# A hybrid decoder block on one NeuronCore: quarter sums of X by adding transfers, X tiles block-major, and four side pieces placed elsewhere

## The chip, the cores and the metric

The kernel runs on one core of a Trainium2 chip. The core has a matmul engine (PE, TensorE, which reads its stationary operand in a weight-load step, PEld), a vector engine (DVE), a scalar engine (ACT), a general engine (POOL), a queue engine (SP) and sixteen DMA engines. Each engine works through its own list of instructions in order. Transfers are issued from the lists of SP, ACT and POOL; a transfer issued by POOL can add what it brings to what is already at its target. The metric is the device time of one execution, in microseconds.

## The reference, cut to what matters

One layer on 1024 tokens of width 1024, all in float32:

```python
hn = rms_norm(h, norm_mix_g)
proj = hn @ w_in                       # gMLP | RG-LRU | SSD z, xBC, dt | gates
ya = gmlp_mixer(za, ...)               # gelu, layer norm, 128x128 mixing, product
yb = rg_lru_mixer(zb, ...)             # conv 4, gates, scan, gelu gate
yc = ssd_mixer(z, xbc, dt_raw, ...)    # softplus(dt), conv 4, chunked scan, norm
gates = sigmoid(g_raw + b_gate)        # three branches
merged = (gates[0] * (ya @ w_branch_a) + gates[1] * (yb @ w_branch_b)
          + gates[2] * (yc @ w_branch_c))
h = h + merged @ w_out
h = h + relu(rms_norm(h, norm_mlp_g) @ w_mlp_up) ** 2 @ w_mlp_down
return rms_norm(h, final_norm_g)
```

In the SSD mixer, `dt = softplus(dt_raw + dt_bias)` and `adt = dt * a` give the decays of 16 heads over 8 chunks of 128 tokens. For each of 4 groups the output is a product inside a chunk plus a product with the state carried from the chunk before.

## The kernel before, in words

Every float32 operand is split into a high half (rounded) and a low half (the rest), and a product is three matmuls: high by high, low by high, high by low. `split` (L125 to L133) makes the halves: ACT writes the high one (L132), DVE subtracts (L133).

**Start.** The rows of x are normalized and transposed; ACT and DVE write X, the transposed input, as sixteen tiles: two halves, two sets of 512 tokens, four pairs of 128-row blocks. Then the value blocks of gMLP run (`v_block`, L257; DVE L236 and L238 end a gelu), and with them the columns for dt.

**Units.** Then come 48 units (`one_unit`, L558). A unit is 48 matmuls (L555) of a 1024x128 weight tile with X, into one of two PSUM buffers (`mainp`). `wtile` (L521) brings the weights: SP loads `raw` (L523), ACT writes high and negated high (L526, L527), POOL issues a transfer that adds `raw` to the latter (L528). Weights are asked for two units ahead. After each unit its `post` reads the PSUM buffer, and `step` advances each waiting generator to its next `yield`. The order of units is four SSD groups of six, each followed by four of the RG-LRU (two heads), then eight of gMLP.

The generators carry the side work. `dt_stages` computes the decays: a softplus on DVE (L218 to L230), adt (L595, L596), then the cumulated sums on TensorE (L601, L602). `ssd_stages` runs a group in two halves of 512 tokens: s1 transposes, s2 states (DVE L720 carries them on), s3 outputs (L729 with the state, L733 inside the chunk; DVE L736 to L739), s4 norm (L746 to L758). The RG-LRU's gate products are L813; their operand is split by L132 and L133. gMLP mixes in L857, L858 evicts, POOL multiplies (L860) and stores (L861).

**Gate pairs.** The 24 blocks of gate columns are made in twelve pairs by a seven-product scheme (Strassen-Winograd): p1 to p7, each of 12 matmuls (`seventh`, L478), on quarters of X and sums of them. T1, T2, T3, T4 are these sums. `x_forms` (L875 to L914) computes them during the gMLP units, with DVE, from high and low quarters (L892 to L905), and splits them. T3 goes back into a quarter of X that is no longer needed. Weight sums and splits of a pair are `Weights` (L484 to L516). The pairs' order is written by hand in `tc.manual_schedule()`.

**Branch products, out projection, MLP.** The branch products are 24 units on Y, the mixers' outputs brought back from memory (`fetch`, `load_next`). Then the weights of the out projection are loaded and split, and for each two row blocks TensorE makes L1142; the rows of x for the residual come by a transfer from ACT's list (L1148), and DVE adds (L1155). Norm, the MLP in the same seven-product scheme, and the final norm follow.

Outside `tc.manual_schedule()` a scheduler of the framework sets the order of each engine's list, with a model of its own for times; the program order is its start. Tiles come from pools of a fixed number of slots (`act` 15, `half` 16, `raw` 2), and an instruction that writes a tile waits until the slot is free.

## Time and profile before

| | us |
|---|---|
| median of 3 runs (2023.78 to 2027.23) | 2026.16 |
| the profiled execution | 2023.37 |
| its span | 2021.7 |
| TensorE busy | 1959.3 (97%) |
| VectorE busy | 1219.6 (60%) |
| ScalarE busy | 944.5 (47%) |
| GpSimd busy | 326.6 (16%) |
| mean granted clock of TensorE | 0.988 |

So 1.7 us of the profiled execution lie outside its span, and the median is 2.8 above it. In the rows of a profile, `out<-in` names what an instruction writes and reads, `xN` counts the instructions of a row, and `[t <-X]` behind a row is idle time of the engine before it and what ended that. In rows of `windows`, busy time of PE, PEld, DVE, ACT and POOL stands in this order, then the granted clock, the mean busy share of the sixteen DMA engines, and GB/s.

### The profile page before, as it was taken

The page shows a single profiled execution, that of the slowest core. Times are in us where ns is not written, and L with a number is a line of the kernel's source. Part 1 is how long each engine was busy: PE and PEld are TensorE (multiplying, and loading weights), DVE is VectorE, ACT ScalarE, POOL GpSimd, SP SyncE. Part 2 cuts the span into 40 slices and gives each one's busy share as a digit, 9 for nine tenths or more (in the row PEclk, how much of TensorE's full clock was granted, in tenths as well). Part 3 has the DMA queues.
Part 4 walks back from the last instruction along what each step waited for, and adds up shares of the span by engine and source line. Part 5 has one row for each costly group of instructions (what it writes and reads, how often), then busy time and mean ns, then how long its engine had stood idle before and what let it go on. Part 6 is the DMA issues. An engine that isn't in the chain of part 4 may idle for free.

```text
span 2021.7 us, 23919 instructions
## 1 busy us (share of the span) xinstructions
PE 1959.3 (97%) x9156; PEld 1633.8 (81%) x9156; DVE 1219.6 (60%) x1796; ACT 944.5 (47%) x1377; POOL 326.6 (16%) x410
## 2 busy tenths in 40 slices
PE   7999999999999999999999999998999999999996
PEld 7997878788788787888878888786788887888885
DVE  5486775765867778444432113336756657787787
ACT  6434665656556534344443222146555555343243
POOL 4112231231322333000000320000111111000000
PEclk9999999999999999999999999999999999999998
DMA  4256456456265564333496665421543448644532
GB/s 157 67 152 129 103 131 138 102 116 129 73 147 119 125 167 134 106 109 114 146 321 186 157 155 136 156 84 63 166 155 132 166 145 309 199 135 136 187 106 92
DMA packets 214887, 285.54 MB, mean 141 GB/s; under 512 B 12548, under 2 KB 149972, under 8 KB 214772
## 3 DMA queue, kind: packets, MB, share of 16 engines
q1 hardware_dynamic: 175636, 144.91, 23.9%
q0 software_dynamic: 33200, 117.59, 22.4%
q10 hardware_dynamic: 5936, 21.51, 3.2%
q8 instruction: 72, 1.18, 0.2%
q14 instruction: 43, 0.35, 0.1%
HBM read 178.97 MB, written 67.24 MB: 122 GB/s over the span
## 4 chain that ended last, share of the span: by engine, by line
PE 78%; DVE 13%; ACT 3%; DMA 3%; issue 2%; POOL 0%; SPq 0%; DVEq 0%; ACTq 0%; POOLq 0%
PE ps L555 32%; PE aux L478 30%; PE gps L478 6%; PE aux L257 3%; PE aux L1142 2%; DVE a L578 1%; PE aux L729 1%; PE aux L733 1%; PE aux L813 1%; DVE rsq_q L111 1%; DMA raw<-in_w_branch_c_dram 1%; DMA a<-in_x_dram 1%; ACT a L1183 1%; DVE a L828 1%; DVE h L750 1%
## 5 line engine op out<-in xcount | busy, mean ns | idle before, releaser
L555 PE MATMUL ps<-xn,wh 128*128 128x512 f32 x1536 | 418.3, 392 | 0.0
L555 PEld LDWEIGHTS ps<-xn,wh 128*128 128x128 f32 x1536 | 286.9, 188 | 61.1 <-issue 2.8
L555 PE MATMUL ps<-xn,wl 128*128 128x512 f32 x768 | 236.6, 389 | 0.0
L478 PE MATMUL aux<-a,b 128*128 128x512 f32 x864 | 197.3, 389 | 0.0
L478 PEld LDWEIGHTS aux<-a,b 128*128 128x128 f32 x864 | 162.2, 188 | 33.7
L526 ACT ACTIVATE wh<-raw 128x1024 fp32r<-128x1024 f32 x72 | 76.0, 1056 | 228.4 <-PE ps L555 201.8
L555 PEld LDWEIGHTS ps<-xn,wl 128*128 128x128 f32 x768 | 144.2, 188 | 30.1
L478 PE MATMUL aux<-b,wt 128*128 128x512 f32 x672 | 156.9, 389 | 0.0
L478 PEld LDWEIGHTS aux<-b,wt 128*128 128x128 f32 x672 | 126.1, 188 | 26.2
L528 POOL DMA_DIRECT2D wl<-raw x72 | 64.0, 889 | 416.4 <-ACT wl L527 248.6
L478 PE MATMUL aux<-b,b 128*128 128x512 f32 x480 | 110.6, 389 | 0.0
L1037 DVE SCALAR_TENSOR_TENSOR a<-a,ps 128x1024 f32<-128x1024 f32 x22 | 26.8, 1220 | 137.9 <-PE ps L555 115.3
L133 DVE TENSOR_TENSOR wt<-a,wt 128x1024 fp32r<-128x1024 f32 x52 | 63.7, 1225 | 72.6 <-ACT wt L132 72.6
L1364 DVE TENSOR_TENSOR a<-aux,a 128x512 f32<-128x512 f32 x112 | 76.8, 687 | 50.5 <-PE aux L478 50.5
L478 PEld LDWEIGHTS aux<-b,b 128*128 128x128 f32 x480 | 90.1, 188 | 18.7
L133 DVE TENSOR_TENSOR a<-a,a 128x1024 fp32r<-128x1024 f32 (+1 forms) x65 | 66.7, 1032 | 47.1 <-ACT a L132 47.0
L132 ACT ACTIVATE b<-wt 128x1024 fp32r<-128x1024 f32 x60 | 61.9, 1053 | 69.6 <-DMA wt<-u_d 53.8
L555 PE MATMUL ps<-c,wh 128*128 128x512 f32 x320 | 85.5, 389 | 0.0
L478 PE MATMUL aux<-a,wt 128*128 128x512 f32 x336 | 78.7, 390 | 3.3 <-ACT a L1241 3.3
L132 ACT ACTIVATE a<-a 128x1024 fp32r<-128x1024 f32 (+1 forms) x65 | 55.8, 875 | 55.5 <-DVE a L1316 44.2
L478 PEld LDWEIGHTS aux<-a,wt 128*128 128x128 f32 x336 | 62.9, 188 | 17.2 <-ACT a L1241 4.2
L527 ACT ACTIVATE wl<-wh 128x1024 fp32r<-128x1024 f32 x72 | 75.7, 1052 | 0.8
(333 smaller groups left out, 3726.1 us busy)
## 6 DMA issues: line engine op xcount, KB each, us to landing
wl<-raw POOLq DMA_DIRECT2D x72, 512.0 KB, 5.2
wt<-u_d SPq DMA_DIRECT2D x54, 512.0 KB
raw<-in_w_in_dram SPq DMA_DIRECT2D x48, 512.0 KB
u_d<-a POOLq DMA_DIRECT2D x48, 512.0 KB, 5.5
g_d<-a POOLq DMA_DIRECT2D x24, 512.0 KB, 2.9
a<-g_d ACTq DMA_DIRECT2D x22, 512.0 KB
rt<-in_w_mlp_up_dram SPq DMA_DIRECT2D x17, 512.0 KB
a<-acs_d POOLq DMA_DIRECT2D x32, 256.0 KB, 7.6
```

The costliest lines, as they stand in the source:

```text
L111: stt(out=q, in0=r, scalar=nh, in1=r, op0=ALU.mult, op1=ALU.mult)
L132: actv(dst_hi, src, AF.Copy)
L133: (eng or nc.vector).tensor_tensor(out=dst_lo, in0=src, in1=dst_hi.bitcast(F32), op=ALU.subtract)
L257: mm(ps[:, :nt], X.tok(a, k, c), wk[k][w], start=(k == 0 and i == 0), stop=(k == KD - 1 and i == 2))
L478: mm(ps, lhs[l][kk], rhs[r][kk], start=(new and n == 0), stop=(n == 11), skip_group_check=not new)
L526: actv(hi, raw, AF.Copy)
L527: actv(lo, hi.bitcast(F32), AF.Copy, scale=-1.0)
L528: nc.gpsimd.dma_start(out=lo, in_=raw, accum_op=ALU.add)
L555: mm(ps[:, hsl(h)], w[wi][:, k, :], a.rhs(ai, k, h), start=(n == 0), stop=(n == 3 * KD - 1))
L1037: stt(out=t, in0=t, scalar=1.0, in1=ps, op0=ALU.add, op1=ALU.mult)
L1142: mm(ps, M.tok(a, k, c), wo[nb][k][w], start=(k == 0 and a + w == 0), stop=(k == KD - 1 and a == 1))
L1364: tt(out=h, in0=ps, in1=h, op=ALU.add)
```

## The change

1. **X tiles** are laid out block by block, (pair's block, token block, token), so that the 512 tokens of one block are contiguous (`tile`, `rhs`, `tok`).
2. **Decays.** The first stage of `dt_stages` is called before the units, not after the first, and one `yield` of two is gone.
3. **SSD outputs.** One more `yield` stands between s2(1) and s3(1) of a group.
4. **x_forms.** T2, T1 and T4 start as copies of a high quarter (six transfers on SP's list), the low quarter is added by transfers on POOL's list (six), T3 to T2 (two), and the negated T2 to T1 and T4 (four). DVE keeps three additions or subtractions for each of T3's two tiles, and the splits; ACT negates T2. T3's split runs once the queue of units is empty, ahead of the last stage.
5. **Branch c.** The second weight tile of the branch products is asked for in the last gate pair behind p6, not in the loop that loads the fourth to eighth block of Y.
6. **Residual rows.** The first two row blocks of x are asked for ahead of the split of the out projection's weights. 25 slots of the pool are passed over, so that the rows lie in slots 25 and 26 of 27.

```diff
--- before.py
+++ after.py
@@ -139,14 +139,14 @@
 
         def tile(self, part, half, kp):
             if (part, half, kp) not in self.t:
-                self.t[part, half, kp] = self.new[half % len(self.new)]((P, 4, 2, P), F32R)
+                self.t[part, half, kp] = self.new[half % len(self.new)]((P, 2, 4, P), F32R)
             return self.t[part, half, kp]
 
         def rhs(self, part, k, half):
-            return self.tile(part, half, k // 2)[:, :, k % 2, :]
+            return self.tile(part, half, k // 2)[:, k % 2]
 
         def tok(self, part, k, c):
-            return self.tile(part, c // 4, k // 2)[:, c % 4, k % 2, :]
+            return self.tile(part, c // 4, k // 2)[:, k % 2, c % 4]
 
     class Whole:
         def __init__(self, hi, lo):
@@ -164,12 +164,12 @@
 
     def x_high(ps, c, q):
         for k in range(4 * q, 4 * q + 4):
-            actv(X.tile(0, c // 4, k // 2)[:, c % 4, k % 2], ps[q][:, k % 4 * P:(k % 4 + 1) * P], AF.Identity, scale=g2c[:, k:k + 1])
+            actv(X.tok(0, k, c), ps[q][:, k % 4 * P:(k % 4 + 1) * P], AF.Identity, scale=g2c[:, k:k + 1])
 
     def x_low(ps, c, q):
         for k in range(4 * q, 4 * q + 4):
-            stt(out=X.tile(1, c // 4, k // 2)[:, c % 4, k % 2], in0=ps[q][:, k % 4 * P:(k % 4 + 1) * P], scalar=g2c[:, k:k + 1],
-                in1=X.tile(0, c // 4, k // 2)[:, c % 4, k % 2].bitcast(F32), op0=ALU.mult, op1=ALU.subtract)
+            stt(out=X.tok(1, k, c), in0=ps[q][:, k % 4 * P:(k % 4 + 1) * P], scalar=g2c[:, k:k + 1],
+                in1=X.tok(0, k, c).bitcast(F32), op0=ALU.mult, op1=ALU.subtract)
 
...
@@ -595,7 +595,6 @@
         ts(out=adt, in0=dt, scalar1=-1.0, scalar2=None, op0=ALU.mult)
         tt(out=adt, in0=adt, in1=na.unsqueeze(1).to_broadcast([P, NCH, 16]), op=ALU.mult)
         yield
-        yield
         adt_f = adt.rearrange("p c h -> p (c h)")
         ps_a = aux()
         mm(ps_a[:, :P], tri, adt_f, start=True, stop=True)
@@ -614,7 +613,9 @@
         nc.gpsimd.dma_start(out=acs_d.rearrange("t r l -> r t l"), in_=acsT)
         yield
 
-    later(dt_stages())
+    decays = dt_stages()
+    next(decays)
+    later(decays)
 
 
     def ssd_units(g):
@@ -770,6 +771,7 @@
         s4_(0)
         yield
         s2_(1)
+        yield
         yield
         s3_(1)
         yield
@@ -871,47 +873,64 @@
 
     XF = {n: [[X.rhs(part, 4 * kh + kk, th) for kk in range(4)] for part in range(2)]
           for n, kh, th in (("B11", 0, 0), ("B21", 1, 0), ("B22", 1, 1), ("T3", 0, 1))}
+    XF.update({n: [[], []] for n in ("T1", "T2", "T4")})
 
     def x_forms():
-        third = []
-        for n in ("T1", "T2", "T4"):
-            XF[n] = [[None] * 4, [None] * 4]
+
+        def quarter(part, kh, th, kp):
+            return X.tile(part, th, 2 * kh + kp).bitcast(F32)
+
+        def plus(out, in_):
+            nc.gpsimd.dma_start(out=out, in_=in_, accum_op=ALU.add)
+
+        def in_halves(name, kp):
+            for k in range(2):
+                pr = half_((P, 4, P), F32R), half_((P, 4, P), F32R)
+                split(pr[0], pr[1], sums[name][kp][:, k])
+                for part in range(2):
+                    XF[name][part].append(pr[part])
+
+
+        first_of = {"T2": (0, 0), "T1": (1, 1), "T4": (1, 0)}
+        sums = {n: [act((P, 2, 4, P)) for _ in range(2)] for n in first_of}
+        for n, (kh, th) in first_of.items():
+            for kp in range(2):
+                nc.sync.dma_start(out=sums[n][kp], in_=quarter(0, kh, th, kp))
+        t3 = []
         for kp in range(2):
-            def quarter(part, kh, th):
-                return X.tile(part, th, 2 * kh + kp).bitcast(F32)
-
-            def in_halves(name, t):
-                for kk in range(2):
-                    pr = half_(dt=F32R), half_(dt=F32R)
-                    for part in range(2):
-                        XF[name][part][2 * kp + kk] = pr[part]
-                    split(pr[0].rearrange("p (c l) -> p c l", c=4), pr[1].rearrange("p (c l) -> p c l", c=4), t[:, :, kk, :])
-
-            third.append(act((P, 4, 2, P)))
-            t3, d, e = third[kp], act((P, 4, 2, P)), act((P, 4, 2, P))
-            tt(out=t3, in0=quarter(0, 1, 1), in1=quarter(0, 0, 1), op=sub)
-            tt(out=e, in0=quarter(1, 1, 1), in1=quarter(1, 0, 1), op=sub)
-            tt(out=t3, in0=t3, in1=e, op=ALU.add)
+            d = act((P, 2, 4, P))
+            tt(out=d, in0=quarter(0, 1, 1, kp), in1=quarter(0, 0, 1, kp), op=sub)
+            tt(out=d, in0=d, in1=quarter(1, 1, 1, kp), op=ALU.add)
+            tt(out=d, in0=d, in1=quarter(1, 0, 1, kp), op=sub)
+            t3.append(d)
             yield
-            tt(out=d, in0=quarter(0, 0, 0), in1=t3, op=ALU.add)
-            tt(out=d, in0=quarter(1, 0, 0), in1=d, op=ALU.add)
-            in_halves("T2", d)
+        for n, (kh, th) in first_of.items():
+            for kp in range(2):
+                plus(sums[n][kp], quarter(1, kh, th, kp))
+        yield
+        for kp in range(2):
+            plus(sums["T2"][kp], t3[kp])
+        yield
+        for kp in range(2):
+            in_halves("T2", kp)
+            actv(sums["T2"][kp], sums["T2"][kp], AF.Copy, scale=-1.0)
+            plus(sums["T1"][kp], sums["T2"][kp])
+            plus(sums["T4"][kp], sums["T2"][kp])
+        yield
+        yield
+        for kp in range(2):
+            in_halves("T1", kp)
+        yield
+        for kp in range(2):
+            pr = act((P, 2, 4, P), F32R), act((P, 2, 4, P), F32R)
+            split(pr[0], pr[1], sums["T4"][kp])
+            for part in range(2):
+                XF["T4"][part] += [pr[part][:, k] for k in range(2)]
+        sums.clear()
+        while queue:
             yield
-            tt(out=e, in0=quarter(0, 1, 1), in1=d, op=sub)
-            tt(out=e, in0=quarter(1, 1, 1), in1=e, op=ALU.add)
-            in_halves("T1", e)
-            yield
-            tt(out=d, in0=quarter(0, 1, 0), in1=d, op=sub)
-            tt(out=d, in0=quarter(1, 1, 0), in1=d, op=ALU.add)
-            pr = act((P, 4, 2, P), F32R), act((P, 4, 2, P), F32R)
-            split(pr[0], pr[1], d)
-            for part in range(2):
-                for kk in range(2):
-                    XF["T4"][part][2 * kp + kk] = pr[part][:, :, kk, :]
-            yield
-        assert not queue
         for kp in range(2):
-            split(X.tile(0, 1, kp), X.tile(1, 1, kp), third[kp])
+            split(X.tile(0, 1, kp), X.tile(1, 1, kp), t3[kp])
 
     class GatePair:
         def __init__(self, br, e):
@@ -1081,6 +1100,7 @@
             else:
                 early.append(fetch("c", 2))
                 load_next("c", 0, early[0])
+                ahead(2)
             z.p3()
             if nxt:
                 nxt.w.cast22()
@@ -1104,8 +1124,6 @@
         early = [fetch("c", k) for k in range(3, KD)]
         for k in range(3, KD):
             load_next("c", k, early[k - 3])
-            if k == 5:
-                ahead(2)
         one_unit()
     del early
     run()
@@ -1121,6 +1139,18 @@
         return aux2p.tile([P, HF], F32, tag="aux2", name=nm("aux2"))
 
 
+
+    skipped = [act() for _ in range(25)]
+    H = []
+
+    def residual(c):
+        h = act()
+        nc.scalar.dma_start(out=h, in_=x[c * P:(c + 1) * P, :])
+        H.append(h)
+
+    for c in range(2):
+        residual(c)
+    del skipped
     wo = [[], []]
     for nb in range(2):
         for k2 in range(4):
@@ -1129,7 +1159,6 @@
             hi, lo = w_pair(nb == 0 and k2 < 3)
             split(hi, lo, raw)
             wo[nb] += [(hi[:, k, :], lo[:, k, :]) for k in range(2)]
-    H = []
     NF = w_up.shape[1] // P
     NS = NF // 2
     h_d = dram.tile([NCH, P, D], F32, name="h_d")
@@ -1143,10 +1172,9 @@
 
     for cp in range(NCH // 2):
         pss = [aux(), aux()]
-        for i in range(2):
-            h = act()
-            nc.scalar.dma_start(out=h, in_=x[(2 * cp + i) * P:(2 * cp + i + 1) * P, :])
-            H.append(h)
+        if cp:
+            for i in range(2):
+                residual(2 * cp + i)
         for ks in (range(KD - 1), (KD - 1,)):
             for i in range(2):
                 out_products(pss[i], 0, 2 * cp + i, ks)
```

The change's lines stand two lines further down from L597 on (L729 is L730 there, L813 is L815, L858 is L860), and more behind `x_forms`.

TensorE at the end of the tenth unit of an SSD and RG-LRU stretch, before (the 128x128 and 64x128 rows are the SSD outputs, L813 the gate products):

```order
L555 MATMUL ps_2508<-xn_555,wl_2227 128x512
L729 MATMUL aux_2563<-a_1741,h_2096 128x128 x2
L733 MATMUL aux_2564<-a_2218,h_2297 64x128 x2
L729 MATMUL aux_2563<-a_1741,h_2489 128x128
L733 MATMUL aux_2564<-a_2218,h_2297 64x128 x2
L733 MATMUL aux_2564<-a_2221,h_2306 64x128 x4
L729 MATMUL aux_2583<-a_1741,h_2096 128x128
...
L555 MATMUL ps_2658<-xn_224,wh_2408 128x512
L555 MATMUL ps_2658<-xn_537,wh_2408 128x512
L813 MATMUL aux_2605<-h_2474,lw_2470 128x512
L813 MATMUL aux_2605<-h_2475,lw_2470 128x512
```

And with the change:

```order
L555 MATMUL ps_2508<-xn_555,wl_2227 128x512
L815 MATMUL aux_2564<-h_2474,lw_2470 128x512
L815 MATMUL aux_2564<-h_2475,lw_2470 128x512
L815 MATMUL aux_2564<-h_2474,lw_2471 128x512
...
L555 MATMUL ps_2617<-xn_224,wh_2408 128x512
L815 MATMUL aux_2592<-h_2478,lw_2470 128x512
...
L555 MATMUL ps_2617<-xn_555,wl_2409 128x512
L730 MATMUL aux_2674<-a_1755,h_2096 128x128 x2
L730 MATMUL aux_2674<-a_1755,h_2489 128x128 x2
L734 MATMUL aux_2675<-a_2218,h_2297 64x128 x4
```

The outputs of the second half of a group stand a whole unit later, and the gate products L815, which stood behind them, now stand where they were.

DVE in the last two gMLP units, before (a_6234 becomes T4, a_6235 is T1, xn_543 takes T3; L502 to L506 are sums of gate weights):

```order
L133 TENSOR_TENSOR xn_543<-a_5900,xn_537 128x1024
L133 TENSOR_TENSOR h_6398<-a_6235,h_6397 128x512
L904 TENSOR_TENSOR a_6234<-xn_239,a_6234 128x1024
L236 SCALAR_TENSOR_TENSOR a_6390<-a_6390,ps_6340 128x1024
L133 TENSOR_TENSOR h_6402<-a_6235,h_6401 128x512
L905 TENSOR_TENSOR a_6234<-xn_246,a_6234 128x1024
L238 SCALAR_TENSOR_TENSOR a_6389<-a_6390,ps_6340 128x1024
L502 TENSOR_TENSOR a_6409<-a_6337 128x512
L503 TENSOR_TENSOR a_6410<-rt_6336,a_6337 128x512
L506 TENSOR_TENSOR a_6409<-a_6409,rt_6336 128x512
L858 SCALAR_TENSOR_TENSOR a_6415<-aux_6416,vh,bs 128x512
```

With the change:

```order
L133 TENSOR_TENSOR xn_543<-a_5898,xn_537 128x1024
L133 TENSOR_TENSOR xn_546<-a_5980,xn_540 128x1024
L236 SCALAR_TENSOR_TENSOR a_6392<-a_6392,ps_6342 128x1024
L238 SCALAR_TENSOR_TENSOR a_6391<-a_6392,ps_6342 128x1024
L502 TENSOR_TENSOR a_6417<-a_6339 128x512
L503 TENSOR_TENSOR a_6418<-rt_6338,a_6339 128x512
L506 TENSOR_TENSOR a_6417<-a_6417,rt_6338 128x512
L860 SCALAR_TENSOR_TENSOR a_6423<-aux_6424,vh,bs 128x512
L507 TENSOR_TENSOR a_6418<-rt_6338,a_6417 128x512
L860 SCALAR_TENSOR_TENSOR a_6423<-aux_6430,vh,bs 128x512
L133 TENSOR_TENSOR a_6439<-a_5890,a_6438 128x1024
L133 TENSOR_TENSOR a_6443<-a_5891,a_6442 128x1024
```

The sums L904 and L905 and T1's splits between L236 and L238 are gone, T3's second split has come in ahead of L236, and two splits of T4 (a_5890, a_5891) stand behind the two L860.

POOL's list early in the gMLP units, with the change (L884 are the adding transfers, xn the low quarters, a_5898 and a_5980 the two tiles of T3):

```order
L863 DMA ya_d<-a_5871 128x1024
L884 DMA a_5886<-xn_230 128x1024
L884 DMA a_5887<-xn_233 128x1024
...
L884 DMA a_5891<-xn_246 128x1024
L528 DMA wl_6002<-raw_5999 128x1024
L845 DMA a_5964<-vn_d 128x8x128
L884 DMA a_5886<-a_5898 128x1024
L884 DMA a_5887<-a_5980 128x1024
L528 DMA wl_6087<-raw_6084 128x1024
```

Before, the list went from ya_d to yc_d, wl and vn_d with none of the L884 rows. Now the transfer that adds the low half of a weight tile (wl_6002) stands behind six of them, and the next (wl_6087) behind the two that add T3 to T2.

## The prediction

> **What bounds the kernel now.** I read the page first, then the list of what TensorE waited for, then the timelines around each wait.
>
> ```profile
> PE 1959.3 (97%) x9156; PEld 1633.8 (81%) x9156; DVE 1219.6 (60%) x1796; ACT 944.5 (47%) x1377; POOL 326.6 (16%) x410
> ```
>
> TensorE (PE) is busy 1959.3 of 2021.7 us. An edit that leaves the matmuls alone can win only idle time, 62 us, and stretches at a lowered clock. These waits are the ones the edits aim at (total, times, longest):
>
> ```profile
> PE aux L729 <- DVE h L720: 8.1, 4, 2.2
> ...
> PE aux L478 <- DVE a L858: 4.5, 1, 4.5
> ...
> PE aux L601 <- DVE adt L596: 2.1, 1, 2.1
> PE aux L1142 <- DVE a L1155: 1.9, 1, 1.9
> PE ps L555 <- DMA wl<-raw: 1.7, 1, 1.7
> ```
>
> They sum to 18.3 us. The rest of the idle time (start, norm chain, tail) is not touched.
>
> **The change part by part**
>
> **X block-major.** The moving operand of the units becomes contiguous. Units on X and branch products, whose operand is contiguous already, stand in the groups (count, busy, mean ns):
>
> ```profile
> L555 PE MATMUL ps<-xn,wh 128*128 128x512 f32 x1536 | 418.3, 392 | 0.0
> ...
> L555 PE MATMUL ps<-c,wh 128*128 128x512 f32 x320 | 85.5, 389 | 0.0
> ```
>
> 392 against 389 ns, and matmuls overlap (a unit's 48 take 10.90 us in a row below, 227 ns each). I take no gain. Were the 3 ns real, 0.8%, the 1536 of this row at 227 ns would win 0.008 × 349 = 2.7 us: the upper end.
>
> **SSD outputs a product later.** At the end of each of four groups TensorE runs two first outputs, waits for the state update L720, then does the rest at a clock that fell in most groups (PE and DVE timelines, then 2-us windows whose last three columns are clock, DMA share, GB/s):
>
> ```profile
> 254.01 0.60 PE L729 MATMUL aux<-a,h 128*128 128x128 f32 x4
> ...
> 264.10 0.62 PE L555 MATMUL ps<-xn,wh 128*128 128x512 f32 x2
> ```
>
> ```profile
> 389.35 0.60 PE L729 MATMUL aux<-a,h 128*128 128x128 f32 x4
> ...
> 392.27 0.77 PE L729 MATMUL aux<-a,h 128*128 128x128 f32 x2 [1.95 <-DVE h L720]
> ...
> 400.74 0.62 PE L555 MATMUL ps<-xn,wh 128*128 128x512 f32 x2
> ```
>
> ```profile
> 390.54 1.29 DVE L133 TENSOR_TENSOR h<-a,h 128x512 fp32r<-128x512 f32 x2 [0.76 <-ACT h L132]
> 391.75 1.61 DVE L720 SCALAR_TENSOR_TENSOR h<-h,etot,aux 128x64 f32<-128x64 f32 x8
> ```
>
> ```profile
> 394.00:396.00 2.00, 2.00 (x14) 1.67 (x11) 0.79 (x2) 1.99 (x2) 0.86 (x1) 0.56 0.12 18
> ...
> 530.00:532.00 2.00, 2.00 (x16) 1.67 (x13) 1.15 (x2) 1.97 (x3) 0.86 (x1) 0.50 0.34 64
> ...
> 666.00:668.00 2.00, 2.00 (x15) 1.45 (x15) 1.75 (x5) 1.98 (x3) 0.61 (x2) 0.50 0.61 113
> ```
>
> The same matmuls took 264.10 − 254.01 = 10.09 us in the first group, at full clock, and 400.74 − 389.35 = 11.39 in the second, although its wait was 0.28 shorter (2.23, the longest, against 1.95). So the lowered clock costs 1.3 + 0.28, about 1.6 us, in three groups of four: 4.8. With the waits' 8.1 the place costs 12.9 in all.
>
> The wait does not simply go. The program order puts the gate products L813 of the RG-LRU at that spot, and they need the low halves that DVE writes just ahead of L720: L133 x2, 390.54 to 391.83. The pair takes about 0.65 each, so the first half stands at 391.2 and the second at 391.8. TensorE arrives at 389.35, waits about 1.9, does six matmuls of about 0.23 (1.4) and waits at most 0.4 for the second. Per group that is a wait of 1.9, at most 2.2, for 1.95 to 2.23 before: 0 to 0.3 won. If DVE reaches L133 sooner than before, up to the whole wait goes: 8.1.
>
> The clock is the larger part. The gap now has matmuls of 512 columns on both sides instead of outputs of 128 columns. Where a gap of this size had wide matmuls around it (L601's and L1142's), the clock held; and the same outputs without a wait, in a group's first half, ran at 1.00 too:
>
> ```profile
> 160.00:162.00 2.00, 0.96 (x6) 0.92 (x7) 1.19 (x3) 1.46 (x2) 0.00 (x0) 1.00 0.00 0
> ```
>
> ```profile
> 1300.00:1302.00 2.00, 1.45 (x6) 1.21 (x7) 1.18 (x2) 0.00 (x0) 0.00 (x0) 1.00 1.02 406
> ```
>
> ```profile
> 210.00:212.00 2.00, 2.00 (x26) 1.71 (x25) 1.45 (x2) 2.00 (x3) 0.00 (x0) 1.00 0.69 206
> ```
>
> I take two of the three drops away: 3.2, with bounds 0 and 4.8. Together 3.8 (bounds 0 to 12.9; and 1 lost, if the moved outputs meet full DVE work a unit later).
>
> The Trainium skill ("TensorE: Matmul & The Clock Gate", its section on the HAM clock gate) has the clock halve after at least one idle window of about 3.4 us and asks for no gaps above that. By it the 1.95-us gap should have cost no clock; the 0.56 after it speaks against the plain reading. By the rule alone this part would win 0.6, not 3.8.
>
> **Sums of quarters by transfers.** The last gMLP outputs are late and two gate products wait for them:
>
> ```profile
> 783.09 5.42 PE L478 MATMUL aux<-xn,wt 128*128 128x512 f32 x12 [4.48 <-DVE a L858]
> ```
>
> ```profile
> 784.00:786.00 2.00, 2.00 (x6) 1.52 (x6) 2.00 (x3) 0.00 (x0) 1.61 (x1) 0.50 0.52 130
> ```
>
> ```profile
> 776.49 1.21 DVE L236 SCALAR_TENSOR_TENSOR a<-a,ps 128x1024 f32<-128x1024 f32 x1
> ...
> 782.30 0.74 DVE L858 SCALAR_TENSOR_TENSOR a<-aux,vh,bs 128x512 f32<-128x512 f32 x1
> ```
>
> The 12 matmuls at clock 0.50 took 5.42, twice what they take at full clock, so the place costs 4.48 + 2.7 = 7.2. The adds that stood before L236 leave DVE, so L236 can start when ScalarE has its input, nearly 2 us sooner. L238, three weight sums and L858 still follow in that order: p2 gets free near 780.6 and waits about 2.1. Then p5 needs S1, whose low half stands on DVE behind L507, L858 and two splits of T4 that have moved there: about 1.5 more. With some chance of the clock falling (0.8 as an estimate), 4.4 remain: 2.8 won (bounds: 7.2 won, if DVE is early enough; losses below).
>
> Its price is 18 transfers of 512 KB.
>
> ```profile
> q1 hardware_dynamic: 175636, 144.91, 23.9%
> q0 software_dynamic: 33200, 117.59, 22.4%
> ...
> wl<-raw POOLq DMA_DIRECT2D x72, 512.0 KB, 5.2
> ```
>
> ```profile
> 700.00:730.00 30.00, 30.00 (x150) 25.45 (x149) 28.76 (x27) 12.33 (x15) 12.62 (x11) 1.00 0.67 174
> ```
>
> 483 us for 144.91 MB is 3.3 us per MB of all sixteen engines on SP's queue, 3.85 on POOL's. Six copies (3.1 MB) and twelve accumulations (6.3 MB) make 10.5 + 24.2 = 35 us in a stretch whose share is 0.67 already. None lies on TensorE's path by itself; what hides them is this slack:
>
> ```profile
> 698.67 0.37 SPq L523 DMA_DIRECT2D raw<-in_w_in_dram  x1
> ```
>
> ```profile
> 727.74 1.21 DVE L236 SCALAR_TENSOR_TENSOR a<-a,ps 128x1024 f32<-128x1024 f32 x1
> ...
> 730.61 1.21 DVE L238 SCALAR_TENSOR_TENSOR a<-a,ps 128x1024 f32<-128x1024 f32 x1
> ```
>
> ```profile
> 736.05 10.90 PE ps L555 x48
> ```
>
> The copies stand on SP behind the load issued at 698.67. T2's first split stands on DVE between this L236 and this L238. TensorE has two PSUM buffers for units, so the unit at 736.05 needs that L238, ended 731.8: 4.2 us of slack. T2 needs a copy, an accumulation and, after T3, a second one; one that accumulates takes 5.2 us to land (the wl<-raw row). T3's first half needs DVE near 719, the second near 727, since SSD's norm (L750 to L757, eight ops and some 8 us) has moved into that stretch. First T2 near 726 to 732, with DVE itself up to 4 us late: just inside the slack. I charge 0.5.
>
> **Decays earlier.** DVE's softplus (25 ops, about 7 us) moves from after the third unit to before the first.
>
> ```profile
> 143.02 3.91 DVE L578 SCALAR_TENSOR_TENSOR a<-ps,scw,a 128x1023 f32<-128x1023 f32 x3
> ...
> 149.51 0.95 DVE L222 RECIPROCAL a<-a 128x128 f32<-128x128 f32 x1
> ...
> 160.70 0.28 DVE L596 TENSOR_TENSOR adt<-adt,na 128x128 f32<-128x128 f32 x1
> ```
>
> ```profile
> 112.00:160.00 48.00, 44.32 (x133) 1.00 0.50 151
> 105.00:112.00 7.00, 3.33 (x10) 1.00 0.54 141
> ```
>
> L601's 2.1 goes. DVE is 92% busy from 112 to 160, with 3.7 us free before it: these absorb their share and 3.3 push all that follows. The first unit's convolution releases its PSUM at 146.9 (143.02 + 3.91). The third unit, which needs it, ended with the wait of L601 at 161.0 − 2.1, so it began at 148.0: slack 1.1, and 0.7 more for decay products that now stand in front. 3.3 − 1.8 is a new stop of 1.5; the value blocks, with no slack that I find, lose 0.3. Net 0.3 won (2.1 won to 2 lost).
>
> **Second branch-c weight.** Now a request late behind others takes 15 us:
>
> ```profile
> 1002.53 15.00 DMA raw<-in_w_branch_c_dram
> ```
>
> Asked for a gate product earlier, it lands in time: 1.7 won, less 0.4 (an estimate) since its two casts stand ahead of a split on ScalarE that the last product wants. 1.3 (0 to 1.7).
>
> **Residual rows.** They are asked for ahead of five weight casts instead of behind them:
>
> ```profile
> 1294.19 5.16 DMA a<-in_x_dram
> ```
>
> Any start 2 us sooner takes away the wait: 1.9 (0 to 1.9; behind it stand the casts, with several us to spare).
>
> **Sum.** 0 + 3.8 + 2.8 − 0.5 + 0.3 + 1.3 + 1.9 = 9.6 us. The profiled execution took 2023.4, so it would take 2013.8. The median shown is 2026.2, 2.8 above it; from there, 2016.6. I forecast 2015.5. A measurement of this kernel tells about 0.2% (4 us) from no change.
>
> **The rivals**
>
> *The clock is not the gap's.* If the drop at the group ends has another cause, or L813 behind a gap brings it too, the 3.2 stay lost: 9.6 − 3.2 = 6.4, about 2019. For it: the drop shows in three of four groups and not at the two other gaps of 2 us. Against: the outputs without a wait stayed at full clock. Chance 0.13. The Trainium skill ("TensorE: Matmul & The Clock Gate", HAM clock gate), read strictly, gives this time as well.
>
> *The gate products' wait vanishes too.* DVE does L133 before TensorE asks; then this place gives its full 12.9 instead of 3.8: near 2006. Against it: what releases L133 is ScalarE's L132, unchanged. Chance 0.06.
>
> *Waits are only exchanged.* L813 waits and the clock falls as before, p2 and p5 give 1, decays lose 1.5, the two requests win 3.2: 2 to 3 us, about 2023, not to be told from no change. Chance 0.17.
>
> *T2 comes late (slower).* The shares of the 16 engines leave about 10 us free from 700 to 730, and copies and accumulations that stand ahead of T2 in the queues want up to 27 (six copies 10.5, eight accumulations 16). If T2's half comes after 733, DVE is held with L238 and the gMLP outputs behind it, and TensorE stops one for one. At 746 that is 13 us, and a lowered clock for 2.7 as at p2; the 2.3 of this part is not won. 9.6 − 2.3 − 13 − 2.7 is 8 us slower, near 2033. From 738 on the whole is no faster than before (9.6 − 2.3 − 2.7 = 4.6 against 738 − 733 = 5). For it: the queues in order (a weight's accumulation on POOL stands behind six others). Against: first copies and first accumulations are T2's own, and other traffic yields too. Chance 0.2.
>
> **Chances.** The forecast has 0.44. Faster: 0.44 + 0.13 + 0.06 = 0.63; same: 0.17; slower: 0.20. Faster cases reach from 2006 to 2021. The range, 2005 to 2030, leaves out the worst of the late T2 and little at the fast end; the forecast's own is 2010 to 2021.
>
> **What would show it.** Right: no wait of L601 on L596, of L555 on an accumulated weight near 1027, of L1142 on L1155; at the group ends a wait of L813 on L133 of 1.5 to 2 us, followed by a clock of 1.00; p2's wait near 2. Wrong: four waits at L813 with a clock of 0.5 behind them; a stop at units between 730 and 765 that ends with a split or L238; the value blocks or the first units waiting on L578; longer casts of weights.

## The result and the profile after

The change took 2034.39 us (median of 5 runs, 2032.85 to 2037.58) against 2026.16 before (5 runs, 2023.78 to 2027.68). The ratio is 1.0044, with a 95% interval of 1.003 to 1.0059: slower by 0.44%, outside the range of the prediction and on its unlikely side. The profiled execution has a span of 2032.6 us, 10.9 more than before. The page says that TensorE did nearly the same work:

```profile
PE 1962.2 (97%) x9156; PEld 1632.6 (80%) x9156; DVE 1200.9 (59%) x1784; ACT 957.4 (47%) x1387; POOL 339.0 (17%) x422
```

Of the five waits that the edits aimed at, four have left its list and p2's has shrunk from 4.5 to 1.0 (the L860 row). Others have come (L815 is L813 of before, L609 the transpose of the decays' sums, L859 gMLP's mixing, L860 is L858, L1056 is L1037):

```profile
PE ps L555 <- DVE a L238: 8.1, 2, 8.0
...
PE aux L815 <- ACT h L132: 4.3, 4, 1.1
PE aux L609 <- DVE w L606: 4.2, 1, 4.2
PE aux L859 <- DMA a<-vn_d: 4.0, 1, 4.0
...
PE ps L555 <- DVE a L1056: 1.7, 1, 1.7
...
PE aux L478 <- DVE a L860: 1.0, 1, 1.0
PE aux L815 <- DVE h L133: 0.9, 4, 0.2
```

The length of each stage, from the starts of its first matmuls in the two PE timelines, tells where the 10.9 us came from:

| stage | before | after | difference |
|---|---|---|---|
| to the first unit | 126.09 | 125.75 | −0.3 |
| units of SSD and RG-LRU | 569.97 | 567.36 | −2.6 |
| gMLP units, to the first pair's p1 | 79.57 | 97.20 | +17.6 |
| the first pair | 15.47 | 11.53 | −3.9 |
| other pairs, to the first branch product | 222.38 | 223.42 | +1.0 |
| branch products | 263.30 | 263.29 | 0.0 |
| out projection to the end | 744.92 | 744.03 | −0.9 |

One stage lost 17.6 us. There the sixteen DMA engines were full: the next rows are 700 to 770 us of the profile before and of the one after (columns as before; the last three are clock, DMA share, GB/s; the view prints shares a little above 1 where the engines are full).

```profile
700.00:770.00 70.00, 70.00 (x351) 59.47 (x350) 53.72 (x52) 25.59 (x29) 27.05 (x22) 1.00 0.61 163
```

```profile
700.00:770.00 70.00, 58.02 (x269) 48.49 (x268) 33.09 (x32) 21.43 (x26) 31.01 (x29) 0.88 1.01 248
...
740.00:750.00 10.00, 2.08 (x5) 1.73 (x6) 8.22 (x8) 5.43 (x7) 6.66 (x7) 0.50 0.79 210
```

Read backwards from TensorE's stop, the timelines of PE, DVE and ACT and the chain of waits of the change say what was late:

```profile
736.20 3.76 PE L859 MATMUL aux<-wT,a 128*128 128x128 f32 x16 [4.02 <-DMA a<-vn_d]
747.92 2.04 PE L555 MATMUL ps<-xn,wh 128*128 128x512 f32 x4 [7.96 <-DVE a L238]
```

```profile
741.78 1.22 DVE L236 SCALAR_TENSOR_TENSOR a<-a,ps 128x1024 f32<-128x1024 f32 x1 [18.23 <-ACT a L235]
```

```profile
738.32 1.06 ACT L526 ACTIVATE wh<-raw 128x1024 fp32r<-128x1024 f32 x1 [25.49 <-DMA raw<-in_w_in_dram]
```

```profile
706.24 31.99 DMA raw<-in_w_in_dram
```

A load of 512 KB of weights, issued behind the six copies, took 32 us. Its cast L526 stands on ScalarE ahead of the square of a gelu (L235) that has its input already. So ScalarE stood idle for 25.5 us, DVE for 18.2, and TensorE ran out of PSUM buffers, although that weight was wanted only two units later.

The same load held GpSimd's list too. The adding transfer of its low half (L528) waited 17.0 us for the cast, and the stores of an SSD output (yc_d) stand behind it. The chain of waits goes this way: L238 starts when that store has landed (an instruction that writes a tile waits until its slot is free).

```profile
741.13 0.85 POOL L528 DMA_DIRECT2D wl<-raw  x1 [17.00 <-ACT wl L527]
```

```profile
742.24 4.40 DMA yc_d<-a
746.64 1.13 DVE a L238
```

DVE's two splits of T2 between L236 and L238 end at the same time, so which of the two came last can't be told. The first 4.0 us of the stop are a wait for another late transfer (vn_d, the values for the mixing, behind the additions on GpSimd's list); without it TensorE would have stood at L238 instead. The stop cost 12.0 us of waiting in all, and behind it the clock stood at 0.50.

### The profile page after: what moved, and what is told of

It reads as the page before. It is cut to its first block, busy times and chain, and to the rows that moved or that the text cites. A ratio compares the mean times of both kernels' runs of the same rounds, so it can differ in the third digit from the quotient of the medians.

```text
span 2032.6 us, 23950 instructions
## 1 busy us (share of the span) xinstructions
PE 1962.2 (97%) x9156; PEld 1632.6 (80%) x9156; DVE 1200.9 (59%) x1784; ACT 957.4 (47%) x1387; POOL 339.0 (17%) x422
## 4 chain that ended last, share of the span: by engine, by line
PE 71%; DVE 12%; DMA 8%; ACT 5%; issue 3%; POOL 1%; SPq 0%; ACTq 0%; POOLq 0%; DVEq 0%
PE aux L478 30%; PE ps L555 27%; PE gps L478 6%; DMA raw<-in_w_in_dram 3%; PE aux L1171 3%; PE aux L257 2%; DVE a L578 1%; DMA wl<-raw 1%; PE aux L815 1%; DVE rsq_q L111 1%; DMA b<-yb_d 1%; DMA raw<-in_w_branch_c_dram 1%; ACT a L1211 1%; DVE a L830 1%; PE aux L734 1%
## 5 line engine op out<-in xcount | busy, mean ns | idle before, releaser
L555 PE MATMUL ps<-xn,wh 128*128 128x512 f32 x1536 | 421.3, 394 | 8.1 <-DVE a L238 8.1
L555 PEld LDWEIGHTS ps<-xn,wh 128*128 128x128 f32 x1536 | 288.6, 189 | 70.2 <-issue 11.0
L555 PE MATMUL ps<-xn,wl 128*128 128x512 f32 x768 | 237.7, 391 | 0.0
L526 ACT ACTIVATE wh<-raw 128x1024 fp32r<-128x1024 f32 x72 | 76.1, 1057 | 249.6 <-PE ps L555 201.2
L555 PEld LDWEIGHTS ps<-xn,wl 128*128 128x128 f32 x768 | 145.3, 189 | 30.7
L528 POOL DMA_DIRECT2D wl<-raw x72 | 63.8, 886 | 412.4 <-ACT wl L527 249.8
L1056 DVE SCALAR_TENSOR_TENSOR a<-a,ps 128x1024 f32<-128x1024 f32 x22 | 26.8, 1220 | 137.7 <-PE ps L555 124.9
L132 ACT ACTIVATE b<-wt 128x1024 fp32r<-128x1024 f32 x60 | 61.8, 1055 | 69.8 <-DMA wt<-u_d 59.7
L555 PE MATMUL ps<-c,wh 128*128 128x512 f32 x320 | 85.5, 389 | 0.0
L578 DVE SCALAR_TENSOR_TENSOR a<-ps,scw,a 128x1023 f32<-128x1023 f32 (+2 forms) x48 | 61.1, 1273 | 39.2 <-ACT a L576 38.5
L132 ACT ACTIVATE a<-a 128x1024 fp32r<-128x1024 f32 (+1 forms) x65 | 55.8, 875 | 58.2 <-DVE a L1344 44.4
```

Source lines behind the costliest of these rows:

```text
L132: actv(dst_hi, src, AF.Copy)
L526: actv(hi, raw, AF.Copy)
L528: nc.gpsimd.dma_start(out=lo, in_=raw, accum_op=ALU.add)
L555: mm(ps[:, hsl(h)], w[wi][:, k, :], a.rhs(ai, k, h), start=(n == 0), stop=(n == 3 * KD - 1))
L578: stt(out=dst[:, j:], in0=ps[:, :T - j], scalar=taps[3 - j], in1=dst[:, j:], op0=ALU.mult, op1=ALU.add)
L1056: stt(out=t, in0=t, scalar=1.0, in1=ps, op0=ALU.add, op1=ALU.mult)
```

## The experiments

Each comparison is against runs of the kernel before on the same chip. Their median is 2027.93 us beside the parts alone except the requests and beside the change without the transfers; 2027.46 beside the requests, the copies from GpSimd's list, the sums three units sooner and the first of the versions that keep what pays; 2027.59 beside the others. Differences are between medians, ratios have 95% intervals.

### Each part alone

**The sums by transfers alone** (with the tiles block-major, which they need):

```diff
 before.py, with class Pairs, x_high, x_low and x_forms as in the change
```

> The kernel before with only the quarter sums by adding transfers (and the block-major tiles they need). Theory: this part alone makes the whole loss. In the profile of the change the stage from the first gMLP mixing to the first gate product took 17.6 us more and the first pair 3.9 less, so 13 to 14 us slower than before, with one load of raw weights that takes about 30 us near 700 to 740, ScalarE idle until it lands, and a lowered clock behind the stop. Rival 1 (the sums themselves are late): about the same time, but DVE's idle time ahead of the stop ends with T2's split, not with ScalarE's square of a gelu. Rival 2 (the loss comes from the parts together, since the SSD norms fall into the same stretch): less than 5 us slower.

2040.79 us, 12.9 slower, ratio 1.0065 (1.0052 to 1.0078). The part makes the loss alone. In its profile units wait three times for L238: 4.0, 1.1 and 4.8 us. Ahead of the first, the weight load holds ScalarE for 20.5 us; ahead of the second, T2's sums hold it for 3.2 and 3.8; ahead of the third, a load of gate weights (rt) holds it for 7.2 and a sum of T1 for 1.9:

```profile
735.29 1.06 ACT L526 ACTIVATE wh<-raw 128x1024 fp32r<-128x1024 f32 x1 [20.47 <-DMA raw<-in_w_in_dram]
...
753.61 0.63 ACT L132 ACTIVATE h<-a 128x512 fp32r<-128x512 f32 x1 [3.84 <-DMA a<-a]
...
767.03 1.06 ACT L132 ACTIVATE wt<-rt 128x1024 fp32r<-128x1024 f32 x1 [7.24 <-DMA rt<-in_w_in_dram]
```

So the first rival holds for a small part: 1.1 of these 9.9 us are T2's, the rest stands mostly behind loads of weights. The load was issued at 712.8 and had landed at 735.3: 22.5 us, less than the 30 expected.

**The change without the transfers:**

```diff
 after.py, with x_forms as before on tiles (P, 2, 4, P)
```

> The change with x_forms as before on DVE (on block-major tiles), all else of the change kept. Theory: 2034.4 less 13.7, near 2020.7, and so 5 us faster than before: the SSD outputs win about 8, the decays lose 3 to 5, the requests win 1 to 2. The stage from the first mixing to the first gate product is again 79 to 81 us, and p2 waits 4 to 5 as before. If the parts collide (SSD norms and the old adds share DVE there), p2's wait or the units lose some us of it, and the time is 2024 or more.

2022.02 us, 5.9 faster, ratio 0.9971 (0.9959 to 0.9983). As the theory had it. p2 waits 4.5 us again, as before, and from 700 to 770 TensorE is busy throughout with a DMA share of 0.63.

**The SSD outputs alone:**

```diff
         s2_(1)
         yield
+        yield
         s3_(1)
```

> The kernel before with only the one more yield ahead of s3(1). Theory from the profile of the change: four waits of 1.3 at the gate products instead of four of 2.0 at the outputs, and the clock stays at 1.00: 8.1 - 5.2 + 4.8 = 7.7 us faster, near 2018.5. Rival (the waits are only exchanged, the clock falls in most groups as before): 2 to 3 us faster. Rival (SSD's norm, a unit later, collides with gMLP's gelus and x_forms on DVE): no gain or a loss, with new waits of units on L238 after 700 us.

2023.21 us, 4.7 faster, ratio 0.9978 (0.9968 to 0.9988). The stage up to gMLP's first mixing took 562.4 us against 569.97 before: 7.6 won where the theory says, and the rival that the clock falls as before is refuted. By the medians 2.9 us of it are missing. The profile, of the slowest of the eight runs (2026.47), gives back more, far behind and at places that the edit doesn't touch: the branch products took 3.6 us more than in the profile before and the rest from the out projection on 5.4 more. There L1143 (L1142 of before) waited 4.1, not 1.9, for a residual row, with a lowered clock behind it.

```profile
1300.62 7.15 PE L1143 MATMUL aux<-wb,b 128*128 128x512 f32 x18 [4.11 <-DVE a L1156]
```

**The decays alone:**

```diff
         yield
-        yield
         adt_f = adt.rearrange("p c h -> p (c h)")
...
-    later(dt_stages())
+    decays = dt_stages()
+    next(decays)
+    later(decays)
```

> The kernel before with only the decays earlier. Theory from the profile of the change: the wait of 2.1 at the sums goes and one of 4.2 at the transpose behind them comes (DVE reaches the difference L606 only behind the layer norms of the value rows), with a lowered clock for 1 to 3 us: 3 to 5 us slower, near 2030. Rival (the prediction's): within 2 us of before.

2032.1 us, 4.2 slower, ratio 1.0017 (1.0008 to 1.0026). DVE comes to what these sums need of it (L602, L606) only behind the layer norms of the value rows, L606 also behind the first of the convolution's three L578, and TensorE's transpose waits:

```profile
137.32 0.38 PE L600 MATMUL aux<-adt,tri 128*128 128x128 f32 x2
...
145.46 0.33 PE L609 MATMUL aux<-ident,acs 128*128 128x128 f32 x1 [4.30 <-DVE w L606]
```

The stage of the units took 575.2 us, 5.2 more than before; with the 7.6 that the SSD outputs win there, this makes the change's −2.6 in the table. In the change, the same stop of 4.24 us is followed by a clock of 0.50 from 146 to 148:

```profile
146.00:148.00 2.00, 2.00 (x6) 1.54 (x5) 2.00 (x8) 0.31 (x1) 0.00 (x0) 0.50 0.94 176
```

**The two requests alone:**

```diff
                 load_next("c", 0, early[0])
+                ahead(2)
...
-            if k == 5:
-                ahead(2)
...
+    for c in range(2):
+        residual(c)
```

> The kernel before with only the two earlier requests (second branch-c weight, two residual rows). Prediction's step: 1.3 + 1.9 = 3.2 us faster. By the profiles since: the wait at the out projection was 1.9 in one profile and 3.0 to 4.1 with a lowered clock in three others, and it goes in all of them (2 to 6 us); the wait for the branch weight comes back as one for a PSUM buffer behind L1037, so nothing from it. 2 to 5 us faster. Rival (given back in the norm chain behind): within 1 us of before.

2021.61 us, 5.9 faster, ratio 0.9974 (0.9964 to 0.9983). Neither L555 near 1027 nor the first out product waits. How the gain falls on the two wasn't measured apart. The branch products took 263.30 us before, 262.23 here and 263.29 in the change, where a wait of 1.7 for a PSUM buffer (L1056) stands in place of the one that went, so most of it seems to be the residual rows. That is more than the 1.9 of the profile before: in three profiles of kernels that leave this place as it was (the sums alone, the SSD outputs alone, the decays alone) the wait is 3.0, 4.1 and 3.2, and the 18 matmuls behind it took 6.0 to 7.2 us, against 4.4 in the profile before.

The earlier branch weight shows no gain. In all ten profiles with this edit a wait for a PSUM buffer of 0.7 to 2.2 us stands in the branch products; in four of them (the kernel with the two good parts, a third of the transfers less, T4 alone, both) the clock falls behind it and the stage takes 265.0 to 265.3 us. A kernel with the residual rows alone wasn't run.

The four parts sum to 12.9 − 4.7 + 4.2 − 5.9 = 6.5 us slower; the change as a whole was 8.2 slower in its own comparison. The block-major tiles weren't timed alone; the kernel that has them and the two good parts (below) is 9.8 faster where these alone sum to 10.6, so no gain of theirs is to be seen.

### What makes the transfers late

**Copies from GpSimd's list:**

```diff
-                nc.sync.dma_start(out=sums[n][kp], in_=quarter(0, kh, th, kp))
+                nc.gpsimd.dma_start(out=sums[n][kp], in_=quarter(0, kh, th, kp))
```

> The change with the six copies issued from GpSimd's list instead of SP's, so that no weight load stands behind them on its queue; as many bytes. Theory A (the engines as a whole are full): the load of the late weight still takes 25 us or more, and the time is near 2034. Theory B (the load is late since it stands behind six copies on SP's queue): it lands within 15 us, the stop on ScalarE goes, what is left is the wait for the sums: 2026 to 2028.

2030.45 us, 3.0 slower than before, ratio 1.0015 (1.0006 to 1.0025); the change was 8.2 slower than its own runs of before. Theory B is right on the weight: L526 no longer waits for it. Theory A is right on the bytes: the DMA share is 1.03, other transfers are late instead, and TensorE has the same stop of 8 us. This time what holds L238 is the store of the SSD output: yc_d, issued on GpSimd's list behind the copies and six of the additions, took 17.4 us to land (median of two; 2.5 before), and DVE stood idle for 14.2 (DVE and PE timelines).

```profile
742.63 1.22 DVE L238 SCALAR_TENSOR_TENSOR a<-a,ps 128x1024 f32<-128x1024 f32 x1 [14.18 <-DMA yc_d<-a]
```

```profile
744.00 2.05 PE L555 MATMUL ps<-xn,wh 128*128 128x512 f32 x4 [8.18 <-DVE a L238]
```

The sum of T2 is late too: it holds ScalarE for 16.5 us. But its split comes at 746.02, two us after TensorE has gone on, so it isn't what stopped TensorE here:

```profile
746.02 1.15 ACT L132 ACTIVATE h<-a 128x512 fp32r<-128x512 f32 x2 [16.48 <-DMA a<-a]
```

**A third of the transfers less** (the low quarters are left out of T1, T2 and T4):

```diff
-        for n, (kh, th) in first_of.items():
-            for kp in range(2):
-                plus(sums[n][kp], quarter(1, kh, th, kp))
```

> The change without the six transfers that add the low quarters (T1, T2 and T4 then hold only sums of the high quarters: this part of the computation is left out), so 12 of 18 transfers. Theory (the sixteen engines are full from 700 to 770 and the last weight and the sums land late): the load of the late weight takes well under 32 us, and of the 13 to 14 us that the transfers cost more than half goes: 2020 to 2027. Rival (not the bytes, but the place of six copies on SP's queue ahead of the weight loads): the load still takes 25 us or more and the time stays above 2030.

2021.92 us, 5.7 faster than before, ratio 0.9975 (0.9966 to 0.9984). That is what the change without any transfer took (2022.0): twelve transfers cost nothing in sum (a stop of 2.3 at L238 against the first pair's gain), and the other six make the difference to the change, 14 us with each kernel against its own runs of before. The share from 700 to 770 is 0.94 here, 1.01 in the change.

```profile
700.00:770.00 70.00, 67.71 (x338) 57.06 (x337) 44.99 (x44) 28.49 (x32) 32.20 (x27) 1.00 0.94 246
```

The rival is refuted: the six copies stand on SP's queue ahead of the weight load as in the change, but the load, issued at 705.5, is there when its cast's turn comes. L526 waits for TensorE to release the slot, not for a transfer:

```profile
719.26 1.06 ACT L526 ACTIVATE wh<-raw 128x1024 fp32r<-128x1024 f32 x1 [6.25 <-PE ps L555]
```

The eight tiles that the sums hold are held here too, so these alone don't make the stop. Whether it is the bytes of the six additions or their place on GpSimd's list isn't told apart.

**The sums three units sooner:**

```diff
+            if h == 6:
+                later(x_forms())
             if h == 7:
                 v_group(0)
...
-            if g == 0:
-                later(x_forms())
-            elif g == 5:
+            if g == 5:
```

> The change with x_forms begun behind the gelu of the seventh RG-LRU head, about three units (35 to 40 us) sooner, all else kept. Theory (the sixteen DMA engines are full from 700 to 770, so the last weights land late and hold ScalarE): the same transfers fall on a stretch that was nearly idle before (share 0.12 from 650 to 660, 0.01 from 680 to 690); the last weight loads land within 15 us, the stop near 735 to 748 is gone, the first pair's gain stays: 2034.4 - 14 to 17, near 2018 to 2020. Rival (such a run of transfers holds whatever weight is next, wherever it stands): a stop of several us near 650 to 710 instead, 2028 or more.

2034.82 us, 7.4 slower than before, ratio 1.0041 (1.0029 to 1.0054). The rival was right: gMLP's stage fell back to 80.4 us and the first pair to 9.5, but the stop moved. Its first part waits for the convolution of the last RG-LRU unit, whose ACT row waits for a tile that a store (yb_d) still reads, and its second for L238 again:

```profile
674.98 0.77 PE L555 MATMUL ps<-xn,wh 128*128 128x512 f32 x1 [11.58 <-DVE a L578]
...
700.44 2.05 PE L555 MATMUL ps<-xn,wh 128*128 128x512 f32 x4 [5.29 <-DVE a L238]
```

```profile
668.67 1.20 ACT L576 ACTIVATE a<-ps,va 128x1024 f32<-128x1024 f32 x1 [4.63 <-DMA yb_d<-a]
```

The store waited 5.6 us to land; how much of the 11.6 is due to the transfers and how much to the eight tiles of `act` that the sums hold (of fifteen) isn't told apart.

### Versions that keep what pays

**SSD outputs, requests and block-major tiles, without the rest:**

```diff
 after.py, with x_forms as before on tiles (P, 2, 4, P), and dt_stages and its call as before
```

> The change with x_forms on DVE as before and the decays as before: block-major tiles, SSD outputs and earlier requests are left. Theory (parts add): 2022.0 of the run without the transfers less 4.2 for the decays, near 2018, 0.5% faster than before. Rival (the parts share a stretch): 2021 or more.

2017.63 us, 9.8 faster, ratio 0.9958 (0.9946 to 0.9971): the parts add.

**T4 alone by transfers**, on that kernel:

```diff
+        t4 = [act((P, 2, 4, P)) for _ in range(2)]
+        for kp in range(2):
+            nc.sync.dma_start(out=t4[kp], in_=quarter(0, 1, 0, kp))
...
+            plus(t4[kp], quarter(1, 1, 0, kp))
...
+            actv(d, d, AF.Copy, scale=-1.0)
+            plus(t4[kp], d)
...
-            tt(out=d, in0=quarter(0, 1, 0), in1=d, op=sub)
-            tt(out=d, in0=quarter(1, 1, 0), in1=d, op=ALU.add)
...
             z.p6()
+            if late_split:
+                t4_split(late_split.pop())
```

> The run without transfers and with the old decays (2017.6), but T4 alone by transfers: two copies, two low quarters, two negated T2, six in all; T1 and T2 on DVE, T4's split behind p6 of the first pair. Theory (a third of the bytes fits beside the rest; DVE ahead of the last gMLP outputs is freed of four adds and the splits of T4 and T3's stand ahead): no stop between 700 and 770, p2's wait falls from 4.5 to 2 or less and the clock holds in part: 3 to 6 us faster than 2017.6, so 2012 to 2015. Rival (every transfer in this stretch delays a weight that holds ScalarE): a stop there, 2018 or more.

2015.99 us, ratio to before 0.9946 (0.9934 to 0.9959); 1.6 below the kernel without transfers, with intervals that overlap. With a third of the bytes nothing stops from 700 to 770, at a share of 0.76, and p2's wait falls to 0.9 with no lowered clock. A new wait of 2.1 in the first pair, for ScalarE, takes part of it back.

```profile
774.07 3.01 PE L478 MATMUL aux<-xn,wt 128*128 128x512 f32 x12 [0.92 <-DVE a L859]
...
793.21 2.98 PE L478 MATMUL gps<-a,a 128*128 128x512 f32 x12 [2.06 <-ACT a L946]
```

**Softplus sooner, sums a unit sooner** (both yields stay), on the kernel without transfers:

```diff
-    later(dt_stages())
+    decays = dt_stages()
+    next(decays)
+    later(decays)
```

> The run without transfers and with the old decays (2017.6), but with the softplus ahead of the units and both yields kept, so that the decays' sums stand behind the second unit, one earlier than before and one later than in the change. Theory (the sums in the change came while DVE still had the layer norm of the last value rows in its list): DVE has caught up, neither the wait of 1.7 to 2.1 at the sums nor the one of 4.2 at the transpose is there: 1 to 2 us faster, near 2016. Rival (DVE, pushed by 7 us, holds the first units' convolutions): a new wait of units on L578, 2018 or more.

2015.87 us, ratio to before 0.995 (0.9937 to 0.9962); 1.8 below, again with intervals that overlap. The wait at the sums is gone, and of the change's 4.2 at the transpose there are 0.5 left.

**Both:**

```diff
 the last two edits on one kernel
```

> T4 alone by transfers and the softplus ahead of the units with both yields, on the run without transfers. If both edits pay and add: 2011 to 2014, faster than both kernels. If either turns into a stop: 2016 or more.

2013.31 us (2011.79 to 2014.32), ratio to before 0.9931 (0.9918 to 0.9945): 14.3 us faster than before, where the change was 8.2 slower than its own runs of before.

## Why the prediction was wrong, point by point

**The step that failed** is the one on the slack of the transfers: "None lies on TensorE's path by itself; what hides them is this slack", with 0.5 us charged. The bytes were counted (35 us of sixteen engines) and the free share too (10 us from 700 to 730), and these numbers did not fit together; the text set only the T2 sum against its slack and left the weight loads to "other traffic yields too". A load that yields has a price: a late load stops an engine not when TensorE wants the weight but when the cast's turn comes in an in-order list, here two units sooner and ahead of a gelu. Stores that land late (yc_d) hold the next writer of their tile in the same way, and the text didn't count them. It also priced the landing of an addition at 5.2 us; in the full stretch it took 12.3 and 9.3 (medians of the low quarters and of the rest). The measured cost of the part is 12.9 us slower where 2.3 faster was forecast.

**The rival of the late T2** had the right root (more transfers than free share) and the right place: a stop at units near 736 to 748 with a lowered clock. It forecast 2033, and 2034.4 was measured. What is late it had wrong: in the change it is the weight load, with the gelu on ScalarE and the store on GpSimd's list behind it, and with the copies off SP's queue it is the store. Where T2's sum was seen to stop TensorE, in the part alone, it took 1.1 us. So that its size came out is luck in part. By its own figures, 27 us wanted and 10 free, it could have had more than a chance of 0.2.

**The Trainium skill** ("DMA: Bandwidth & Descriptors", "Issuing engines are not separate DMA queues") says that transfers started from ScalarE, SP and GpSimd run on the same sixteen engines. The runs agree: with the copies moved to GpSimd's list the share was 1.03, and another transfer was late. But the time against before went from 8.2 slower to 3.0, so the list still mattered for which transfer was late, and for what that cost.

**First pair.** 2.8 forecast, 3.9 measured; p2 waited 1.0, not 2.1, and p5 1.2, with the clock at 1.00.

**SSD outputs.** 3.8 forecast; the stage won 7.6, of it 2.6 from the waits (8.1 to 5.5 in the part alone) and the rest, some 5, from the clock. That both would gain was right, the reasons were not. The wait at the gate products was 1.1 + 0.2 per group, not 1.9: the first of them needs only the high half, which ScalarE (L132) has ready before DVE has the low one, and runs while the latter is made. And the clock held: in windows around the ends of the groups it is 1.00 in 39 of 39 cases (the change and nine experiments with this edit, but for one group that lies in the stop of the earlier sums), and below 1 in 13 of 16 for the four kernels with the old order. The forecast gave the wide matmuls on both sides as the reason, with a gap as long as before. Wide matmuls didn't keep the clock: five gaps of 1.87 to 2.18 us between matmuls of 512 columns in the branch products lowered it. This one is of the kernel with the two good parts; the four matmuls behind it took 2.04 us:

```profile
1053.77 2.04 PE L555 MATMUL ps<-a,wh 128*128 128x512 f32 x4 [2.13 <-DVE a L1038]
```

```profile
1054.00:1056.00 2.00, 2.00 (x5) 1.56 (x6) 0.00 (x0) 0.38 (x1) 0.43 (x1) 0.50 0.78 188
```

The length of the gap does separate the cases. In the fourteen profiles, from 100 to 1360 us, the mean clock of the 3 us behind a wait of TensorE is 1.00 for all 69 waits of 0.9 to 1.85 us, below it for 20 of 29 of 1.87 to 2.36, and for all 20 of 3.0 to 5.3. So the gap's fall to 1.1 is enough to explain the gain, and a gap of 1.9, as forecast, would likely have cost the clock: that this term came out is luck. What decides between 1.87 and 2.36 stays open. Gaps of 1.95 lowered the clock and 1.3 did not; the Trainium skill's 3.4 us ("TensorE: Matmul & The Clock Gate", HAM clock gate) would have let both pass.

**Decays.** 0.3 faster forecast, 4.2 slower measured. The push of DVE was seen, the place where it bites was not: the text looked at the first unit's convolution (L578), but the sums' own evictions (L602, L606) stand on DVE behind the pushed layer norms, and TensorE's transpose waits for them. With the sums one unit later the same edit was 1.8 faster by the medians, which their intervals don't settle.

**Requests.** 3.2 forecast, 5.9 measured. The branch weight's wait came back as one for PSUM (1.7), which the text didn't have; the residual rows' wait is larger in most runs than in the one profile from which it was priced.

**Sum.** Of 9.6 us, the parts that were forecast at 7.0 (SSD outputs, requests) gave 10.6; the two others, forecast at 2.6, cost 17.1.

## What to carry to other kernels

When transfers take over an engine's work, put their time on all DMA engines beside the free share of the stretch, and where the sum goes over one, ask for every transfer in it, stores too, which in-order list waits for its landing, and what stands behind in that list. A prefetch has slack only until its first consumer (here a cast) is at the head of its engine's list. And price a wait of a kernel from several profiles where a transfer ends it: one profile gave 1.9 us for a place that cost 3 to 4 in others.

## What was not expected of the hardware

The loss set in between a share of 0.94 and one of 1.01 (700 to 770 us): with twelve transfers the time was that of none, with eighteen it was 14 us more. An addition of 512 KB between two tiles took 12.3 us to land (median of the six for the low quarters) in the full stretch. The weights' own addition wl<-raw, also 512 KB between tiles, took 8.1 there, 5.5 in the same stretch before and 5.2 in the median over the whole kernel before. And gaps of TensorE of 1.9 us already lowered its clock in most cases, between wide matmuls as between narrow ones.
